# The first FFN projection by tokens, in block products with 512 and 384 moving weight columns, and activations turned on TensorE

## The chip, the cores and the metric

The kernel runs on one core of a Trainium2 chip. A core has a matrix engine (TensorE, PE), three engines for elementwise work (VectorE or DVE, ScalarE or ACT, GpSimd or POOL) and queues for DMA transfers, of which SyncE's (SP) carries nearly all loads here. The engines run side by side and wait for each other through semaphores. The metric is the device time of one execution in microseconds, as the median of several runs.

## What is computed

One layer of a streaming encoder over 512 tokens of 1024 features, in float32. The part that the change touches is the feed-forward network at the end:

```python
    h = h + (g_a * ya + g_b * yb) @ w_o[l]
    hn = rmsnorm(h, norm_ffn_g[l])
    gu = hn @ w_ffn_in[l]
    g, up = jnp.split(gu, 2, axis=-1)
    h = h + (jax.nn.silu(g) * up) @ w_ffn_out[l]
    return rmsnorm(h, final_norm_g)
```

`w_ffn_in` has 1024 rows and 2 x 2816 columns, `w_ffn_out` 2816 rows and 1024 columns. Ahead of it come one combined projection, a gated recurrence with a convolution, and a band attention with 16 heads.

## The kernel before

**Three matmuls for a product.** Each float32 operand is split into a high part (rounded to the type fp32r) and a low part, the rest. A product of two such operands is high x high + high x low + low x high, three matmuls (`mm3`, lines 76 to 78). A split is one ACT copy (line 82) and one DVE subtraction (line 83). A matmul holds a block of 128 x 128 (the stationary operand) and streams the columns of the other (the moving operand), at most 512, through it.

**Block products.** The larger products are cut into 2 x 2 blocks and computed with seven block products instead of eight (Strassen's method in Winograd's form). It needs sums of blocks on both sides, made on DVE, and a few copies and additions of partial results.

**The projection before.** For each pair of 128 features of the gate half ("fg", j = 0, 2 .. 20) and of the up half ("fu"), two loads of 512 KB bring 1024 x 256 weights. `weight_sums` (line 182) makes four sums of 512 elements per partition and splits seven blocks into tiles of the pool `wp` (tag "whl", four buffers) and of others. `block_product` (line 452) runs seven products of 4 x 3 matmuls with the weights held and 256 tokens moving, keeps partial results with ACT (line 460), and adds them on DVE (lines 472 and 473). The results have features on partitions, which is what the second projection wants; SiLU (line 1381) and a multiplication (line 1386) make the activations. The first pair, "fg0" and "fu0", is computed plainly, without blocks, in halves of 256 tokens: `project_half` (line 1297), 8 x 3 matmuls for each of 4 tiles and 2 halves. That covers the norm of the second half of the tokens: `norm_half` (line 526) scales the rows (line 532), turns them on PE (line 543), and writes high parts (line 545, ACT), low parts (line 547, DVE) and the whole values (line 550, ACT) of the features; sums of these blocks (lines 1325 to 1339) are the moving side of the block products. The sums for "fg2" are begun ahead (line 1276).

**What sets the order.** PE runs in an order written by hand from the attention to the norm (`manual_schedule`), and again, with DVE, in the second projection; elsewhere a planner orders each engine by simulated times, except where `keep_in_program_order` fixes an instruction. Weights are prepared ahead by `prefetch`, up to the chunk named by `barrier`. Loads go through SP in order; a raw tile (pool `wp`, three buffers) must be free first.

**Around it.** `v_all` (line 1013) computes the attention's values by tokens: activations are held and 512 weight columns move, in seven block products of 2 x 4 x 3 matmuls, over two weight tiles per kind, of the four "whl" buffers. The output projection `w_o` works in the same way (`o_product`, line 1226); two of its four weight sums, and the parts of two others, are made early, in the recurrence, by `o_weight_sums` (line 353) and kept in DRAM. In the second projection five feature pairs are computed plainly (`plain`, after `split_act`) and six by blocks (`paired`, after `a_first` and `a_sums`).

Of the kernel before, what the change touches and what calls it, by code (L numbers as in the profile page):

```python
# [38 lines left out]
def block_kernel(ctx: ExitStack, tc: tile.TileContext, x, norm_mix_g, w_in, b_merge, rel_table,  # L39
# [54 lines left out]
    strassen = [f"f{w}{j}" for j in range(2, FT, 2) for w in "gu"]  # L94
# [33 lines left out]
    for j in range(0, FT, 2):  # L128
        plan(f"fg{j}", cols(w_ffn_in, j * P))
        plan(f"fu{j}", cols(w_ffn_in, DFF + j * P))  # L130
# [27 lines left out]
    def load(name, k):  # L158
# [4 lines left out]
        pl, bufs = wp, 3  # L163
        if name in strassen and name[0] == "f":
            loads[0] += 1
            pl, bufs = (room[0], 1) if loads[0] % 4 == 0 and loads[0] > 4 else (wp, 3)
        raw = pl.tile([P, n, wide], F32, tag="raw", bufs=bufs, name=f"raw_{name}_{k}")
# [7 lines left out]
    slots, loads = [0], [0]  # L175
    barrier = ["o_w11"]
    room = [None]

    begun = {}
    spare = [None]  # L180

    def weight_sums(name, ahead=False):

        def blocks_of():
            for k in (0, 4):
                if (name, k) not in raws:
                    load(name, k)
            r0, r1 = raws.pop((name, 0)), raws.pop((name, 4))
            return r0[:, :, 0:P], r0[:, :, P:CW], r1[:, :, 0:P], r1[:, :, P:CW]

        if name not in begun:
            a11, a21, a12, a22 = blocks_of()
            s21, s34 = (sums_room.tile([P, 2, 4, P], F32, tag=tag, bufs=1, name=f"{tag}_{name}")
                        for tag in ("s21", "s34"))
            s2, s1, s3, s4 = s21[:, 0], s21[:, 1], s34[:, 0], s34[:, 1]
            first_sum = dve.tensor_add(s1, a21, a22)
            if name == "fu2":

                tc.keep_in_program_order(first_sum)
            dve.tensor_sub(s2, s1, a11)  # L200
            dve.tensor_sub(s3, a11, a21)
            dve.tensor_sub(s4, a12, s2)
        if ahead:
            slots[0] += 1
            o = sums_room.tile([P, 2, 2, 4, P], F32R, tag="whl", bufs=1, name=f"whl_{name}_s2")
            split(o[:, :, 0], o[:, :, 1], s21[:])
            begun[name] = (s34, {"s2": o[:, 0], "s1": o[:, 1]})
            return
        sc = room[0]
        blocks_ = {}  # L210
        if name in begun:

            a11, a21, a12, a22 = blocks_of()
            s34, blocks_ = begun.pop(name)
            s1 = s2 = None
            s3, s4 = s34[:, 0], s34[:, 1]
        for group in ((("a11", a11), ("a12", a12)), (("s2", s2), ("s1", s1)), (("s3", s3), ("s4", s4)), (("a22", a22),)):
            if group[0][0] in blocks_:
                continue
            if name == "fg2" and group[0][0][0] == "a":  # L220

                for key, src in group:
                    o = spare[0].tile([P, 2, 4, P], F32R, tag="act", bufs=13, name=f"whl_{name}_{key}")
                    split(o[:, 0], o[:, 1], src)
                    blocks_[key] = o
                continue
            pl, tag, bufs = sc, "a22", 2
            if len(group) == 2:
                slots[0] += 1
                pl, tag, bufs = (sums_room, "whl", 1) if slots[0] % 5 == 1 else (wp, "whl", 4)  # L230
            o = pl.tile([P, len(group), 2, 4, P], F32R, tag=tag, bufs=bufs, name=f"whl_{name}_{group[0][0]}")
            together = group[0][0] in ("s2", "s3")
            if together:
                split(o[:, :, 0], o[:, :, 1], (s21 if group[0][0] == "s2" else s34)[:])
            for i, (key, src) in enumerate(group):
                if not together:
                    split(o[:, i, 0], o[:, i, 1], src)
                blocks_[key] = o[:, i]
        return blocks_
# [106 lines left out]
    o_sums = {n: dr.tile([2, P, D], F32, name=f"o_t{n}") for n in (1, 2)}  # L346
    o_parts = {n: dr.tile([2, P, 2 * D], F32, name=f"o_hl{n}") for n in (3, 4)}

    def o_block(dst, kh, half, u):
        at = kh * S + u * CW  # L350
        sp.dma_start(out=dst, in_=w_o[at:at + CW, half * S:half * S + S].rearrange("(k p) e -> p k e", p=P))

    def o_weight_sums(pl, u):

        tiles = [pl.tile([P, 2, S], F32R, tag=f"b{n}", name=f"o_b{n}_{u}")[:] for n in range(4)]
        b11, b12, b21, b22 = (f(b) for b in tiles)
        for n, b in enumerate((b11, b12, b21, b22)):
            o_block(b, n // 2, n % 2, u)
# [4 lines left out]
        for n, hi, b in ((1, tiles[1], b12), (2, tiles[3], b22)):  # L363
            sp.dma_start(out=o_sums[n][u], in_=b.rearrange("p k e -> p (k e)"))
        for n, hi, lo in ((3, tiles[1], tiles[0]), (4, tiles[3], tiles[2])):
            act.activation(hi, f(lo), AF.Copy)
            dve.tensor_sub(lo, f(lo), f(hi))
            for part, o in enumerate((hi, lo)):
                sp.dma_start(out=o_parts[n][u][:, part * D:(part + 1) * D], in_=f(o).rearrange("p k e -> p (k e)"))
# [82 lines left out]
    def block_product(name, i, right, c):  # L452
# [6 lines left out]
        def keep(o, src):  # L459
            act.activation(o, src, AF.Copy)  # L460
# [1139 lines left out]
```

## Time and profile before

| What | Value |
|---|---|
| Median of 3 runs | 853.36 us (853.11 to 853.51) |
| The profiled execution | 853.5 us |
| Its span, first to last instruction | 851.7 us |
| Read from HBM | 105.97 MB |

All times of single instructions are of the one profiled execution; its span is 1.8 us shorter than its time as measured from outside. A row of a timeline gives the start of an instruction in the span, its duration in us, the engine, the line of the kernel, the operation, the tiles written and read, and how many followed in a row (x). A row of a window gives for each engine the time in which it was busy and how many instructions touched the window; PEclk is the granted share of TensorE's clock, and the last two columns are the busy share of the DMA engines and GB/s. A row of a group gives busy time and mean duration of one in ns, then the idle time of the engine before these instructions and what ended it. A row of waits names who waited, for whom, and the total, the times and the longest in us.

### The profile page before, as it was taken

Reading aid. Unit: us, or ns where it says so; the run is one execution under the profiler, and the core shown is the slowest. Engines: PE = TensorE matmul, PEld = TensorE weight load, DVE = VectorE, ACT = ScalarE, POOL = GpSimd, SP = SyncE. Lnnn points to the kernel's source line nnn. Section 1 sums busy time; section 2 is a strip of 40 time slices with the busy share of each in tenths; the row PEclk is TensorE's granted clock in tenths of the full one; section 3 lists DMA queues with packets and bytes.
Section 4 is the critical chain, followed back from the end, with each engine's and each line's share of the span. In section 5 each row is a group of like instructions: output and inputs, shape, how many; then the busy total and the mean of one; then the engine's idle time right before and its main releaser. Section 6 shows DMA issues by size and latency. Waiting matters only on the chain.

```text
span 851.7 us, 13103 instructions
## 1 busy us (share of the span) xinstructions
PE 841.7 (99%) x4890; PEld 742.0 (87%) x4890; DVE 662.9 (78%) x1032; ACT 521.0 (61%) x913; POOL 99.8 (12%) x161
## 2 busy tenths in 40 slices
PE   8999999999999999999999999999999999999996
PEld 6988888888888888888888889999999999888885
DVE  6667769777958788887578687898888787798785
ACT  7595848774356688787643477556556557545434
POOL 2412030221110133233000000000000001000000
PEclk9999999999999999999999999999999999999999
DMA  9433386432724433232233861433333333337432
GB/s 293 157 105 118 125 295 247 117 100 90 229 63 146 130 93 100 75 88 62 76 122 118 320 240 49 142 104 120 100 99 105 98 107 104 123 131 239 160 125 99
DMA packets 96670, 115.24 MB, mean 135 GB/s; under 512 B 6520, under 2 KB 78800, under 8 KB 96096
## 3 DMA queue, kind: packets, MB, share of 16 engines
q1 hardware_dynamic: 94976, 110.90, 40.9%
q10 hardware_dynamic: 1232, 2.95, 0.9%
q8 instruction: 38, 0.62, 0.3%
q0 software_dynamic: 400, 0.57, 0.2%
q14 instruction: 24, 0.20, 0.1%
HBM read 105.97 MB, written 8.43 MB: 134 GB/s over the span
## 4 chain that ended last, share of the span: by engine, by line
PE 97%; DVE 1%; ACT 1%; DMA 0%; issue 0%; ACTq 0%; DVEq 0%
PE po_out L76 2%; PE po_out L77 2%; PE po_out L78 2%; PE o L1130 2%; PE p_fu L78 2%; PE p_fg L78 2%; PE p_fg L77 2%; PE p_fg L76 2%; PE p_fu L77 2%; PE p_fu L76 2%; PE pT L1110 2%; PE po_gb L76 2%; PE po_xr L76 2%; PE po_xr L77 2%; PE po_ga L78 2%; PE po_q L76 2%
## 5 line engine op out<-in xcount | busy, mean ns | idle before, releaser
L1099 POOL TENSOR_SCALAR p<-p,rl 128x128 f32<-128x128 f32 (+3 forms) x61 | 37.5, 635 | 16.5 <-DVE rl L1095 15.8
L1094 ACT ACTIVATE p<-p,m 128x128 f32<-128x128 f32 (+1 forms) x64 | 35.5, 555 | 5.2 <-DVE m L1093 4.9
L1371 POOL TENSOR_TENSOR act_lo<-act,act_hi 128x1024 fp32r<-128x1024 f32 x1 | 2.4, 2408 | 299.3 <-ACT act_hi L1370 299.3
L1093 DVE CUSTOM_DVE_ANT_0 p<-s,bias 128x128 f32<-128x128 f32 (+1 forms) x64 | 28.6, 486 | 11.1 <-PE s L1085 9.2
L76 PE MATMUL po_out<-whl_fo,act_hi 128*128 128x512 f32 (+1 forms) x80 | 30.8, 385 | 0.5 <-ACT c_u L460 0.5
L78 PE MATMUL po_out<-whl_fo,act_lo 128*128 128x512 f32 (+1 forms) x80 | 30.7, 384 | 0.0
L77 PE MATMUL po_out<-whl_fo,act_hi 128*128 128x512 f32 (+1 forms) x80 | 30.7, 384 | 0.0
L83 DVE TENSOR_TENSOR whl_fu_s<-s_fu,whl_fu_s 128x1024 fp32r<-128x1024 f32 x20 | 24.2, 1222 | 6.3 <-ACT whl_fu_s L82 6.3
L83 DVE TENSOR_TENSOR whl_fg_s<-s_fg,whl_fg_s 128x1024 fp32r<-128x1024 f32 x20 | 24.1, 1223 | 5.7 <-ACT whl_fg_s L82 5.7
L83 DVE TENSOR_TENSOR pp<-pT,pp 128x384 fp32r<-128x384 f32 (+1 forms) x48 | 26.9, 595 | 2.0 <-ACT pp L82 1.8
L77 PE MATMUL po_xr<-xnT,whl_xr 128*128 128x512 f32 (+1 forms) x80 | 27.7, 353 | 0.0
L77 PE MATMUL po_gr<-xnT,whl_gr 128*128 128x512 f32 (+1 forms) x80 | 27.5, 347 | 0.0
L78 PE MATMUL po_gr<-xnT,whl_gr 128*128 128x512 f32 (+1 forms) x80 | 27.3, 347 | 0.0
L78 PE MATMUL po_xr<-xnT,whl_xr 128*128 128x512 f32 (+1 forms) x80 | 27.2, 346 | 0.0
L76 PE MATMUL po_gr<-xnT,whl_gr 128*128 128x512 f32 (+1 forms) x80 | 27.1, 347 | 0.0
L76 PE MATMUL po_xr<-xnT,whl_xr 128*128 128x512 f32 (+1 forms) x80 | 26.3, 351 | 0.4 <-ACT xnT L658 0.4
L76 PE MATMUL po_k<-xnT,whl_qk 128*128 128x512 f32 x64 | 25.5, 398 | 0.0
L76 PE MATMUL po_q<-xnT,whl_qk 128*128 128x512 f32 x64 | 25.5, 398 | 0.0
L76 PE MATMUL po_ga<-xnT,whl_ga 128*128 128x512 f32 x64 | 25.4, 397 | 0.0
L76 PE MATMUL po_gb<-xnT,whl_gb 128*128 128x512 f32 x64 | 25.2, 394 | 0.0
L78 PE MATMUL po_ga<-xnT,whl_ga 128*128 128x512 f32 x64 | 25.0, 391 | 0.1
L77 PE MATMUL po_ga<-xnT,whl_ga 128*128 128x512 f32 x64 | 25.0, 390 | 0.0
(603 smaller groups left out, 3267.1 us busy)
## 6 DMA issues: line engine op xcount, KB each, us to landing
raw_fg<-in_w_ffn_in_dram SPq DMA_DIRECT2D x24, 512.0 KB, 4.0
raw_fu<-in_w_ffn_in_dram SPq DMA_DIRECT2D x22, 512.0 KB, 3.5
raw_qk<-in_w_in_dram SPq DMA_DIRECT2D x32, 256.0 KB, 3.2
raw_fo<-in_w_ffn_out_dram SPq DMA_DIRECT2D x16, 512.0 KB, 3.4
raw_xr<-in_w_in_dram SPq DMA_DIRECT2D x8, 512.0 KB, 5.6
raw_gr<-in_w_in_dram SPq DMA_DIRECT2D x8, 512.0 KB, 4.3
raw_ga<-in_w_in_dram SPq DMA_DIRECT2D x8, 512.0 KB, 3.8
raw_gb<-in_w_in_dram SPq DMA_DIRECT2D x8, 512.0 KB, 3.7
```

Of the source, the lines that this page charges most:

```text
L76: pe.matmul(o, sh, mh, start=start, stop=False, skip_group_check=parts)
L77: pe.matmul(o, sh, ml, start=False, stop=False, skip_group_check=parts)
L78: pe.matmul(o, sl, mh, start=False, stop=stop, skip_group_check=parts)
L83: dve.tensor_sub(lo, src, f(hi))
L1093: dve.tensor_tensor_reduce(prob[qb][:], scs[qb][:, 0:w], bias[:, S - w:S], -1.0, 3e38, ALU.add, ALU.min, nmax[:, qb:qb + 1])
L1094: act.activation(prob[qb][:], prob[qb][:], AF.Exp, bias=nmax[:, qb:qb + 1], scale=-1.0, accum_out=lsum[:, qb:qb + 1])
L1099: eng.tensor_scalar(prob[qb][:], prob[qb][:], rl[:, qb:qb + 1], 1.0, ALU.mult, ALU.mult)
L1110: pe.transpose(pt[:, at * P:(at + 1) * P], prob[qb][:, kb * P:(kb + 1) * P], ident[:])
L1130: pe.matmul(po[:, S - n:S], st, pp[i][:, part, lo:lo + n], start=kb == 0 and part == 0, stop=kb == NT - 1 and part == 1)
L1371: (dve if i else pool).tensor_sub(lo[:], o[:], f(hi[:]))
```

## The change

The first projection is computed by tokens, like V and `w_o`: activations are held, weights move. The columns of each half are cut into three units, "fg0", "fu0", "fg1" .. "fu2": 1024 columns in the first two, as two sides of 512, and 768 in the last, as two sides of 384. Each unit runs seven kinds of block products, 2 banks x 4 x 3 matmuls each, with `f_weights` preparing one kind ahead: two loads per kind (four for w11, none for t1 and t4), the sums t1 and t2 in tiles of their own, and two splits into two of the four "whl" tiles. Blocks that are used twice are loaded twice.

The first unit has another order of kinds: w11 and w21, which read the first half of the tokens alone, stand first, while the second half is normalised. Its weight sums are made early by the helper that did so for `w_o`: one half after the last group of the recurrence, the other after the first key tile, and kept in DRAM (t1, t2, t3 whole, t4 in parts). The norm of the second half takes its features in the order 4, 6, 0, 2, with a quarter of a product between the groups. The block for the first half of the features and the second half of the tokens is no longer split, since no product reads it; of the first four `mT` tiles only half is split.

SiLU and the multiplication with the up half work on tiles of 128 tokens (`gated`), the multiplication mostly on GpSimd. Then PE turns the activations, four transposes of 128 x 128 per feature tile and one ACT copy, two tiles at a time behind the first four products of the next gate unit, and the last six tiles at the start of the second projection. There the splits of plain pairs 2 to 4 and the tasks for the six block pairs are spread anew.

The core of the difference:

```diff
-    for j in range(0, FT, 2):
-        plan(f"fg{j}", cols(w_ffn_in, j * P))
-        plan(f"fu{j}", cols(w_ffn_in, DFF + j * P))
+    f_units = [f"f{w}{n}" for n in range(3) for w in "gu"]
+    f_first = ("w11", "w21", "t4", "t1", "t2", "w22", "t3")
+    for unit in f_units:
+        for kind in f_first if unit == f_units[0] else v_kinds:
+            plan(f"{unit}_{kind}")
...
+    kept_sums = {(w, n): dr.tile([2, P, D], F32, name=f"{w}_t{n}") for w, n in (("o", 1), ("o", 2), ("f", 1), ("f", 2), ("f", 3))}
+    kept_parts = {(w, n): dr.tile([2, P, 2 * D], F32, name=f"{w}_hl{n}") for w, n in (("o", 3), ("o", 4), ("f", 4))}
...
+        if (w, kind) == ("f", "t4"):
+            hl = [[sums_room.tile([P, 2, S], F32R, tag=f"t{1 + u}{part}", bufs=1, name=f"whl_f_t4_{u}{part}") for part in range(2)]
+                  for u in range(2)]
+            for u in range(2):
+                for part in range(2):
+                    sp.dma_start(out=f(hl[u][part][:]).rearrange("p k e -> p (k e)"), in_=kept_parts[w, 4][u][:, part * D:(part + 1) * D])
+            return lambda part, k: hl[k // 2][part][:, k % 2]
...
+        pl, bufs = (room[0], 1) if f_loads[0] % 4 == 0 and room else (wp, 3)
+        raw = pl.tile([P, 2, S], F32, tag="raw", bufs=bufs, name=f"raw_{unit}_{kind}_{kh}{side}{u}")
+        at, col = kh * S + u * CW, "gu".index(unit[1]) * DFF + int(unit[2]) * 2 * S + side * wide
+        sp.dma_start(out=raw[:, :, 0:wide], in_=w_ffn_in[at:at + CW, col:col + wide].rearrange("(k p) e -> p k e", p=P))
...
+    def f_weights(unit, kind):
+
+        hl = [wp.tile([P, 2, 2, S], F32R, tag="whl", bufs=4, name=f"whl_{unit}_{kind}_{u}")[:, :, :, 0:f_side(unit)]
+              for u in range(2)]
+        for u in range(2):
+            if kind in ("t1", "t4"):
+                src = f_sums[1 if kind == "t1" else 2, u]
+            elif kind == "t2":
+                ins = f_sum(unit, 2, u, f_raw(unit, kind, 1, 1, u), f_sums[1, u])
+                if u == 0:
+                    tc.keep_in_program_order(ins)
+                src = f_sums[2, u]
+            elif kind == "t3":
+                src = f_raw(unit, kind, 0, 0, u)
+                ins = dve.tensor_sub(src, f_sums[2, u], src)
+                if u == 0:
+                    tc.keep_in_program_order(ins)
+            else:
+                src = f_raw(unit, kind, int(kind[1]) - 1, int(kind[2]) - 1, u)
+            split(hl[u][:, 0], hl[u][:, 1], src)
+            if kind == "w11":
+                f_sum(unit, 1, u, f_raw(unit, kind, 0, 1, u), src)
+            if kind == "w21":
+                dve.tensor_sub(f_sums[2, u], src, f_sums[2, u])
...
-        if j in (2, 4):
-            o_weight_sums(obp, j // 2 - 1)
-    ob_stack.close()
+        if j:
+            sums_kept(obp, "oof"[j // 2 - 1], (0, 1, 0)[j // 2 - 1])
...
     k_tile(0)
+    sums_kept(obp, "f", 1)
+    ob_stack.close()
...
-        split_pair(mT[j], ta[j])
+        at = low_ if j < 4 else every
+        split(mT[j][:, 0, at], mT[j][:, 1, at], ta[j][:, at])
...
+    f_rows = {"w11": (0, 0), "w21": (1, 0), "t4": (1, 1), "t1": "s1", "t2": "s2", "w22": "s4", "t3": "s3"}
...
+        for a in of:
+            at = slice(a * P, (a + 1) * P)
+            for k in ks:
+                mm3(banks[a], src[:, 0, k, at], src[:, 1, k, at], w(0, k), w(1, k), start and k == 0, k == 3, parts=True)
...
+            o = sg[2 * half + a, side]
+            if unit[1] == "g":
+                if keep:
+                    dve.tensor_add(o, banks[a], keep[a])
...
+            else:
+                if keep:
+                    dve.tensor_add(keep[a], banks[a], keep[a])
+                (pool if keep and (unit != f_units[-1] or side) else dve).tensor_mul(o, o, keep[a] if keep else banks[a])
...
+            pt = mm_tile(f"pt_act{j}", "t" if n == 2 and i == 2 else "s")
+            for t in range(NT):
+                pe.transpose(pt[:, t * P:(t + 1) * P], sg[t, side][:, i * P:(i + 1) * P], ident[:])
+            act.activation(act_tile(j // 2)[:, j % 2], pt[:], AF.Copy)
...
+    f_product(fx, "fg0", "w11", True)
+    kept(x1, fx)
+    norm_half(x32p, ht, hsq, gf, hn_at, 1, "ffn", f_at, None, first_products, (4, 6, 0, 2), turned_in)
+    f_product(fy, "fg0", "w21", True, of=(1,), ks=(2, 3))
+    gated("fg0", 0, 0, fy, x1)
...
+    x_sum("s1", dve.tensor_add, lambda i: of_x(0, 1, i), lambda i: of_x(1, 1, i))
...
+    f_product(fz, "fg0", "t4", True)
+    kept(y4, fz)
...
+    fz = f_banks("fg0", "t", "t")
+    f_product(fz, "fg0", "t1", True)
+    kept(z1, fz)
...
+        f_product(fx, unit, "w11", True)
+        kept(x1, fx)
+        turn()
+        f_product(fz, unit, "t1", True)
+        kept(z1, fz)
+        turn()
+        f_product(fx, unit, "t2", False)
+        kept(x2, fx)
+        turn()
+        if last:
             split_act(0)
+        f_product(fz, unit, "w22", False)
+        gated(unit, 0, 1, fz, x2)
+        turn()
+        if last:
+            split_act(1)
+        f_product(fx, unit, "t3", False)
+        gated(unit, 1, 1, fx, z1)
+        fy = f_banks(unit, "y", "t")
+        f_product(fy, unit, "w21", True)
+        gated(unit, 0, 0, fy, x1)
+        f_product(fx, unit, "t4", False, 2 if last else 1)
+        gated(unit, 1, 0, fx)
+        if unit[1] == "u":
+            turns += turns_of(n, sg)
+    turn(3)
+    in_order.close()
...
-            spread(todo, 2 if i < plain[-1] else len(todo))
+            if i + 2 in plain:
+                split_act(i + 2)
+            if i == 0:
+                turn(3)
+                sc_stack.close()
+                bt_stack.close()
+                hn_stack.close()
+                ohp.append(ctx.enter_context(pool_of("act_hi", 1, "right")))
+                out_room[0] = ctx.enter_context(pool_of("out", 1, "right"))
+                barrier[0] = None
+            else:
+                spread(todo, 3)
```

358 lines of the change are left out of this document (142 added, 216 removed).

## The prediction, made before the changed kernel was run

> **What bounds the kernel now.** I read the page from its first part down: busy shares, slices, then the waits of TensorE (PE).
>
> ```profile
> PE 841.7 (99%) x4890; PEld 742.0 (87%) x4890; DVE 662.9 (78%) x1032; ACT 521.0 (61%) x913; POOL 99.8 (12%) x161
> ...
> PE   8999999999999999999999999999999999999996
> ```
> ```profile
> PE busy L486 <- DVE eps_t L492: 1.2, 1, 1.2
> PE po_out L76 <- ACT c_u L460: 0.5, 1, 0.5
> PE po_xr L76 <- ACT xnT L658: 0.4, 2, 0.2
> ```
>
> PE is busy in 841.7 of 851.7 us, and nearly all of the rest lies before its first and after its last matmul: the waits add up to a few us in all. So the time is PE's work, and the question is how long PE takes for the new instruction list and whether the others still keep it fed. In a busy PE the mean duration is no price, since neighbours overlap; the price is the step from one start to the next. The windows and the timeline give it:
>
> ```profile
> core 0: us, PE busy (x) PEld busy (x) DVE busy (x) ACT busy (x) POOL busy (x), PEclk, DMA share, GB/s
> 425.00:480.00 55.00, 55.00 (x244) 45.54 (x243) 44.22 (x71) 25.32 (x37) 0.00 (x0) 1.00 0.47 158
> 560.00:720.00 160.00, 160.00 (x1336) 160.00 (x1335) 134.99 (x186) 95.30 (x172) 2.41 (x1) 1.00 0.34 103
> ```
> ```profile
> 494.74 0.39 PE L76 MATMUL o_x<-whl_o_t,ms 128*128 128x512 f32 x1
> ...
> 498.60 0.39 PE L78 MATMUL o_x<-whl_o_t,ms 128*128 128x512 f32 x1
> 498.83 0.27 PE L543 MATMUL pt_ffn_0t<-ident,xs_ffn 128*128 128x128 f32 x1
> ...
> 499.59 0.27 PE L543 MATMUL pt_ffn_2s<-ident,xs_ffn 128*128 128x128 f32 x1
> ...
> 506.42 0.28 PE L76 MATMUL po_f<-hn,whl_fg 128*128 128x256 f32 x1
> ...
> 511.70 0.28 PE L78 MATMUL po_f<-hn,whl_fg 128*128 128x256 f32 x1
> ```
>
> 18 matmuls of 512 columns start within 3.86 us: 3.86/17 = 0.227 us each. 45 of 256 columns within 5.28 us: 0.120 each. Eight transposes: 0.76/7 = 0.109. The windows agree (160 us over some 1334 matmuls in the FFN, 55 over some 242 in an all-512 stage), at a full granted clock. So two matmuls of 256 cost 0.240 where one of 512 does the same columns in 0.227: about 13 ns of each matmul do not scale with its columns, and the weight-load row says the same (160.00 of 160 us busy in the FFN, 45.54 of 55 in the other stage). That is what this change can win.
>
> **The change, part by part.** *Matmuls.* Before: 20 column pairs of 7x4x3 = 84 matmuls and the first pair plain with 192, all of 256 columns: 1872 x 0.120 = 224.6 us. After: 6 units of 7 products x 2 banks x 4 x 3 = 168 matmuls; four units of 512 columns (672) and two of 384 (336). For 384 the attention has a step:
>
> ```profile
> 305.20 0.34 PE L1084 MATMUL s<-kh,q 128*128 128x384 f32 x1
> 305.37 0.34 PE L1085 MATMUL s<-kl,q 128*128 128x384 f32 x1
> 305.55 0.39 PE L1084 MATMUL s<-kh,q 128*128 128x512 f32 x1
> ```
>
> 0.17 to 0.18; I take the middle of the other two steps, 0.1735. 672 x 0.227 + 336 x 0.1735 = 152.5 + 58.3 = 210.8. Saved: 13.8 us.
>
> *Turning.* The products now come out with tokens on partitions, the second projection wants features there: 22 feature tiles x 4 = 88 transposes are new.
>
> ```profile
> 280.18 1.09 PE pT L1110 x10
> 289.26 1.12 PE pT L1110 x10
> ```
>
> In the attention ten in a row take 1.09 to 1.12 on the chain, so 0.11 each with the change of kind: 88 x 0.11 = 9.7 us. They come in some 12 groups; a group between matmuls may cost up to 0.05 more, 0.6. The transposes of the norm are as many as before.
>
> *A stall that goes.* At the end of the FFN PE waits 0.5 us for the last eviction (second row of the waits). Now the turn of three tiles and a plain output group, 4 x 6 x 0.227 = 5.4 us, stand between the last product and what needs it. What is late next is the multiply of the last bank, two of under 0.7 us: covered. -0.5.
>
> Sum: -13.8 + 9.7 + 0.6 - 0.5 = **-4.0 us**, as long as PE stays fed.
>
> *Feeding PE: DVE and ACT.* A 512 unit (168 x 0.227 = 38.1 us) needs on DVE 14 low parts and 8 sums of 1024 and 6 adds out of PSUM, in an up unit 2 multiplies besides:
>
> ```profile
> L83 DVE TENSOR_TENSOR whl_fu_s<-s_fu,whl_fu_s 128x1024 fp32r<-128x1024 f32 x20 | 24.2, 1222 | 6.3 <-ACT whl_fu_s L82 6.3
> L473 DVE TENSOR_TENSOR c_u<-q_fu,keepa_fu 128x512 f32<-128x512 f32 x10 | 6.9, 688 | 3.1 <-PE q_fu L78 2.1 <-ACT keepa_fu L460 0.8
> L82 ACT ACTIVATE whl_fu_s<-s_fu 128x1024 fp32r<-128x1024 f32 x20 | 20.8, 1054 | 4.2 <-PE q_fg L78 2.2 <-PE q_fu L78 1.7 <-DVE s_fu L202 0.2
> ```
>
> 22 x 1.22 + 6 x 0.69 = 31.0 (up: 32.4) of 38.1, 81 to 85%; in the window above DVE already works 134.99 of 160 (84%) without a single PE wait. ACT: 14 x 1.05, 6 copies, 8 SiLUs or 8 evicted turns of about 0.6: some 23 to 28 of 38. No fuller than now, so the shares cost nothing; the order can. Four weight tiles hold two kinds, so a kind can be split only while the one before it runs: 5.4 us (384: 4.2) for high, low, high, low: 1.05 + 2 x 1.22 = 3.5 at best, 5.9 where two sums stand in between. The V stage runs the same scheme without a PE wait. I take 0; the other end is rival C.
>
> *GpSimd.* 16 multiplies and the low parts of activation pairs 0 to 2 (one there before) go to POOL. They wait for adds, and a turn asks for them one product later. Nearest row:
>
> ```profile
> L773 POOL TENSOR_TENSOR xch<-xc,xch 128x512 fp32r<-128x512 f32 x8 | 11.7, 1466 | 23.1 <-issue 13.0 <-ACT xch L772 10.1
> L83 DVE TENSOR_TENSOR whl_ga<-raw_ga,whl_ga 128x1024 fp32r<-128x1024 f32 x8 | 11.9, 1497 | 2.4 <-ACT whl_ga L82 2.4
> ```
>
> 1.5 us each, hidden. In the stage where POOL does this, DVE's low parts take 1.50 instead of 1.22. The Trainium skill, "GPSIMD Engine Reference" (section "Specifications"), has the reason: GpSimd shares SBUF interfaces with VectorE, with contention where a VectorE instruction has two SBUF inputs; the row agrees. Six such multiplies in an up unit slow perhaps 8 low parts by 0.28: 2.2 us of DVE, from 85 to 91%. Cost 0 with the slack, part of rivals B and C.
>
> *DMA.*
>
> ```profile
> raw_fg<-in_w_ffn_in_dram SPq DMA_DIRECT2D x24, 512.0 KB, 4.0
> raw_fu<-in_w_ffn_in_dram SPq DMA_DIRECT2D x22, 512.0 KB, 3.5
> ```
>
> From the second unit on 12 raw loads per unit instead of one pass: 5 x 12, and 16 for the first, against these 46. 6.3 MB in 38.1 us is 165 GB/s, against 103 above, over three raw tiles and every fourth in a tile of its own. The stage before the FFN shows what PE stands (next rows). Cost 0.
>
> *Sums kept early.* The first unit's weight sums are made in the recurrence and after the first keys: 8 loads, 10 stores, 10 DVE and 2 ACT instructions, with SP's later weight loads queued behind stores that wait for DVE. The same helper already does this for w_o, twice.
>
> ```profile
> 105.00:125.00 20.00, 20.00 (x90) 16.57 (x89) 14.49 (x17) 10.77 (x15) 7.77 (x4) 1.00 0.86 316
> 165.00:200.00 35.00, 35.00 (x156) 29.00 (x155) 23.23 (x29) 24.91 (x35) 6.96 (x10) 1.00 0.40 119
> 460.00:500.00 40.00, 40.00 (x182) 33.20 (x182) 29.22 (x48) 19.53 (x32) 0.00 (x0) 1.00 0.72 267
> ```
>
> At 105 to 125 the chip does exactly that for w_o, at 316 GB/s, and PE is busy throughout. At 165 to 200 DVE has 11.8 us free for 10 x 1.22 = 12.2 us; the rest delays V's sums a little, needed 40 us later. Cost 0; cover gone, about 1 us.
>
> *The FFN's start.* Before, 72 matmuls (8.6 us) cover the second half's norm, now 24 x 0.227 = 5.4.
>
> ```profile
> 506.22 0.68 DVE L200 TENSOR_TENSOR s_fg<-s_fg,raw_fg 128x512 f32<-128x512 f32 x1
> ...
> 507.67 0.68 DVE L202 TENSOR_TENSOR s_fg<-raw_fg,s_fg 128x512 f32<-128x512 f32 x1
> ...
> 509.11 1.22 DVE L83 TENSOR_TENSOR whl_fg_s<-s_fg,whl_fg_s 128x1024 fp32r<-128x1024 f32 x1
> ...
> 510.51 1.40 DVE L532 TENSOR_SCALAR xs_ffn<-h,rs_ffn 128x1024 f32<-128x1024 f32 x2
> ...
> 517.57 1.42 DVE L1325 TENSOR_TENSOR sum_t<-x 128x512 f32<-128x512 f32 x2 [0.17 <-ACT x L550]
> ...
> 520.12 1.22 DVE L1339 TENSOR_TENSOR bt<-sum_t,bt 128x1024 fp32r<-128x1024 f32 x1 [1.12 <-ACT bt L1338]
> ```
>
> PE would reach the transposes at 511.4, the scaled rows are done at 511.9; but the two sums and the split for "fg2" ahead of them on DVE, 2.6 us, are gone. Cost 0 to 0.5.
>
> ```profile
> 515.47 0.27 PE L543 MATMUL pt_ffn_2s<-ident,xs_ffn 128*128 128x128 f32 x1
> ```
>
> From these transposes (515.7) to a split sum (521.3) are 5.6 us; after the change PE has, from its last transposes, 6 + 24 matmuls, 6.8 us, before it needs s1. Covered by about 1 us. One of the norm's four blocks is no longer split, nor half of the first four mT tiles: a little less for ACT and DVE, off PE's path.
>
> *The output's start.* Low parts of pairs 3 and 4 (2.4 us of DVE; pair 2's on POOL) move behind the FFN, and twelve tasks spread over four plain groups, not five.
>
> ```profile
> 740.00:760.00 20.00, 20.00 (x90) 16.57 (x89) 18.02 (x34) 10.30 (x15) 0.00 (x0) 1.00 0.45 151
> ```
>
> DVE is at 18.02 of 20 there; 2.4 us more in five groups of 5.4 still fits, since what comes last is first read by the sixth. SP's loads from "fo0_3" on open one group later and have two more to land. Cost 0; cover gone, up to 2.4.
>
> **The sum.** The profiled execution took 853.5 us (span 851.7), the median shown is 853.36; the difference is nothing here. 853.4 - 4.0 = **849.4 us**.
>
> **The rivals.** A measurement of this kernel tells about 0.2% from no change, 1.7 us. *A, the forecast:* PE stays fed, 849.4, alone 848 to 851. For it: 84% of DVE and no wait now. Chance 0.65.
>
> *B, the covers are a little short:* 0.5 at the scaled rows, 1.5 at s1, 0.3 in each of five units: +3.5, so 852.9, from 851 to 854. For it: the cover at s1 is about 1 us, and six POOL multiplies per up unit slow DVE. Against it: PE is at 160.00 of 160 us today with engines as full. 0.20, mostly within 0.2%.
>
> *C, the two-kind weight buffer becomes the bound (slower):* if sums cannot run ahead, a kind with two sums takes 5.9 us against 5.4 of product; four of seven kinds in five units are such: 20 x 0.45 = 9, so 858.4. It decides once raw weights land later than the start of the product before, so that sum and split stand in a row; landing takes 3.5 to 4.0 us by the page's DMA issues and the raw tiles come free some 5 us ahead. Against it, V. 0.12.
>
> *D, the change does not do what its shapes say:* a transpose holds PE for its duration, 0.275 us, instead of its step: 88 x 0.275 = 24.2, so 863.9. Against it the rows of ten in 1.1 us. The Trainium skill, "TensorE: Matmul & The Clock Gate", Part 4, gives a transpose about 275 ns in a kernel's context; the duration agrees, the step here is 0.11. The same page, "Back-to-back issue gap", puts N/2.4 + 2.5 ns on a warm matmul: by it, as an estimate, 1872 x 109.2 = 204.4 against 672 x 215.8 + 336 x 162.5 = 199.6, a saving of 4.8 alone, and with the transposes the change would lose. As a mechanism of this kernel: were the part that does not scale 2.5 instead of 13 ns, the saving would shrink to about a third and the sum be +5, 858. The steps of 0.120 and 0.227 speak against it. Both 0.03.
>
> **How the numbers follow.** Faster: A and a quarter of B, 0.70. Within 0.2% (851.7 to 855.1): the rest of B, 0.15. Slower: C and D, 0.15. The range: down to 848.0 (transposes at 0.109, no cost of a group, 384 at 0.170), up to 853.8 with nearly all of B; C and D left out.
>
> **What would show it.** Right: matmuls of the projection at 128x512 in steps of 0.227, the stage some 4 us shorter, no PE waits by the projection's products; DVE at about 80% there. B would show as PE waits on the split sums or on norm transposes; C as PE waits on weight tiles, once per heavy kind; D as steps of transposes near 0.275. Wrong would be a wait that grows before the FFN, by the stores in SP's queue.

## The result, and the profile after

The kernel after takes **859.75 us** (median of 7 runs, 858.30 to 863.98); the kernel before took 853.40 beside it (853.11 to 853.88). The ratio is 1.0082 (95% interval 1.0063 to 1.0101): slower by 0.8%, where 849.4 was forecast. The profiled execution of after is the longest of the seven, 863.98 us, with a span of 862.2.

First the busy row, what HBM moved, and PE's waits of the kernel after (who waits, for whom: total, times, longest in us).

```profile
PE 844.7 (98%) x4114; PEld 712.7 (83%) x4114; DVE 662.3 (77%) x972; ACT 519.7 (60%) x864; POOL 140.9 (16%) x179
...
HBM read 122.75 MB, written 13.67 MB: 158 GB/s over the span
```
```profile
PE v_z L77 <- DVE whl_v_t L83: 3.5, 1, 3.5
PE o_z L78 <- DVE ms L83: 1.9, 1, 1.9
PE fu_x L77 <- DVE whl_fu_t L83: 1.6, 1, 1.6
PE fg_x L77 <- DVE whl_fg_t L83: 1.3, 2, 0.7
...
PE fg_y L77 <- DVE whl_fg_w L83: 0.4, 1, 0.4
```

The five rows shown are new, six waits in all, each for a low part that DVE makes (one more new row, of 0.3 us in the attention, is not). The two largest lie in stages whose products the change does not touch: V (`v_z`) and the output projection (`o_z`). DVE is no fuller than before (77% against 78%): what changed is when it gets to the piece that PE wants. The 0.5 us for `c_u` is gone, as forecast.

Three landmarks cut the span: the first matmul of the o stage (the output projection `w_o`), the first transpose of the FFN's norm, the last matmul. Their rows in PE's timeline, of before and then of after:

```profile
466.18 0.39 PE L76 MATMUL o_x<-whl_o_w,mT 128*128 128x512 f32 x1
...
844.84 0.28 PE L78 MATMUL po_last<-whl_fo,act_lo 128*128 128x256 f32 x1
```
```profile
472.53 0.39 PE L76 MATMUL o_x<-whl_o_w,mT 128*128 128x512 f32 x1
...
509.01 1.04 PE L494 MATMUL pt_ffn<-ident,xs_ffn 128*128 128x128 f32 x8
...
855.39 0.28 PE L78 MATMUL po_last<-whl_fo,act_lo 128*128 128x256 f32 x1
```

With the row at 498.83 that the prediction shows: up to the o stage +6.35, in the o stage 36.48 against 32.65 (+3.83), from the norm to the end 346.38 against 346.01 (+0.37). So in this execution 10.2 us are lost before the changed products begin, and their gain of 4 does not show either. The medians are some 6 us apart: the other executions of after lost less. Each part is followed back to what holds DVE.

**V.** DVE's timeline of after, and then PE's (start, duration, and in brackets the idle time before and what ended it):

```profile
245.86 0.16 DVE L1049 RECIPROCAL rl<-l 128x4 f32<-128x4 f32 x1
249.60 1.41 DVE L272 TENSOR_TENSOR raw_v_t<-v_t,raw_v_t 128x1024 f32<-128x1024 f32 x1 [3.58 <-DMA raw_v_t<-in_w_in_dram]
250.93 1.21 DVE L83 TENSOR_TENSOR whl_v_t<-v_t,whl_v_t 128x1024 fp32r<-128x1024 f32 x1
```
```profile
248.28 0.39 PE L76 MATMUL v_z<-whl_v_t,v_s1h 128*128 128x512 f32 x1
252.20 0.50 PE L77 MATMUL v_z<-whl_v_t,v_s1h 128*128 128x512 f32 x1 [3.53 <-DVE whl_v_t L83]
...
253.22 0.63 PE L77 MATMUL v_z<-whl_v_t,v_s1h 128*128 128x512 f32 x1
253.65 0.63 PE L78 MATMUL v_z<-whl_v_t,v_s1l 128*128 128x512 f32 x1
```

The low part that PE waits for (250.93) needs nothing that is late. It stands behind the sum for **t3** (line 272), which no product wants before three more have run, and that sum waits 3.58 us for a raw tile that was still landing. Behind the wait PE's steps are 0.43 instead of 0.227, at a granted clock of 0.53 (window 252.5 to 256.0 us): half clock. What made the stage tight is, by the trace, a row in ACT's timeline 40 us earlier:

```profile
208.20 0.59 ACT L907 ACTIVATE kh<-po_k 64x512 fp32r<-64x512 f32 x1 [6.18 <-DMA f_hl<-f_b]
```

A copy of the second key tile waits 6.18 us for the store of the last kept sums of the first unit, whose memory it takes over.

**The o stage.** DVE's timeline, and two rows of the DMA issues from 455 to 530 us (count, KB each, median us to landing):

```profile
475.21 0.68 DVE L83 TENSOR_TENSOR mT<-za,mT 128x512 fp32r<-128x512 f32 x1
480.70 0.69 DVE L1193 SCALAR_TENSOR_TENSOR h<-o_x,h 128x512 f32<-128x512 f32 x1 [4.81 <-PE o_y L77]
...
487.26 0.68 DVE L83 TENSOR_TENSOR ms<-za,ms 128x512 fp32r<-128x512 f32 x1
```
```profile
whl_f_t<-f_hl SPq DMA_DIRECT2D x4, 512.0 KB, 7.1
h<-in_x_dram ACTq DMA_DIRECT2D x4, 512.0 KB, 10.8
```

The first h add waits 4.81 us, and the `ms` splits that the t1 product wants stand behind it. The bracket names a step of `o_y`, which this add does not read, and the `o_x` product that it does read had ended by 478.2 us. So it was another input: h, whose loads take a median of 10.8 us to land beside the four new loads of t4 parts. They were issued from 472.7 us on, and the quickest took 7.9 us, which gives 480.6.

**The FFN.** Its waits (1.6, 1.3, 0.4) are for low parts in fg1, fg2 and fu2.

### The profile page after: what moved, and what is told of

It reads as the page before. It is cut to its first block, busy times and chain, and to the rows that moved or that the text cites. A ratio compares the mean times of both kernels' runs of the same rounds, so it can differ in the third digit from the quotient of the medians.

```text
span 862.2 us, 11589 instructions
## 1 busy us (share of the span) xinstructions
PE 844.7 (98%) x4114; PEld 712.7 (83%) x4114; DVE 662.3 (77%) x972; ACT 519.7 (60%) x864; POOL 140.9 (16%) x179
## 3 DMA queue, kind: packets, MB, share of 16 engines
HBM read 122.75 MB, written 13.67 MB: 158 GB/s over the span
## 4 chain that ended last, share of the span: by engine, by line
PE 68%; DVE 13%; DMA 11%; ACT 4%; issue 4%; DVEq 0%; ACTq 0%; SPq 0%
DMA raw_fu_w<-in_w_ffn_in_dram 3%; PE po_out L76 2%; PE po_out L77 2%; PE po_out L78 2%; PE o L1084 2%; PE pT L1064 2%; DMA raw_fg_w<-in_w_ffn_in_dram 2%; PE po_ga L78 2%; PE po_ya L76 2%; PE po_ya L77 2%; PE po_ya L78 2%; PE po_ga L76 2%; PE po_ga L77 2%; DMA raw_fu_t<-in_w_ffn_in_dram 1%; PE po_xr L77 1%
## 5 line engine op out<-in xcount | busy, mean ns | idle before, releaser
L1282 POOL TENSOR_TENSOR sg<-sg,keep_fu_x 128x512 f32<-128x512 f32 (+1 forms) x10 | 18.3, 1853 | 240.4 <-DVE keep_fu_x L1281 240.4
L1053 POOL TENSOR_SCALAR p<-p,rl 128x128 f32<-128x128 f32 (+3 forms) x61 | 42.7, 718 | 15.6 <-DVE rl L1049 14.8
L83 DVE TENSOR_TENSOR whl_fo<-raw_fo,whl_fo 128x1024 fp32r<-128x1024 f32 x16 | 20.7, 1303 | 8.0 <-ACT whl_fo L82 8.0
L82 ACT ACTIVATE whl_fu_t<-t_fu 128x1024 fp32r<-128x1024 f32 (+1 forms) x18 | 17.6, 985 | 13.0 <-PE fu_x L78 8.7
L76 PE MATMUL po_ga<-xnT,whl_ga 128*128 128x512 f32 x64 | 25.5, 398 | 0.0
L1275 ACT ACTIVATE sg<-sg 128x512 f32<-128x512 f32 (+1 forms) x20 | 11.9, 596 | 22.4 <-DVE sg L1274 22.0
L78 PE MATMUL po_ga<-xnT,whl_ga 128*128 128x512 f32 x64 | 25.0, 391 | 0.1
## 6 DMA issues: line engine op xcount, KB each, us to landing
raw_qk<-in_w_in_dram SPq DMA_DIRECT2D x32, 256.0 KB, 3.1
```

Of the source, the lines that this page charges most:

```text
L76: pe.matmul(o, sh, mh, start=start, stop=False, skip_group_check=parts)
L78: pe.matmul(o, sl, mh, start=False, stop=stop, skip_group_check=parts)
L82: act.activation(hi, src, AF.Copy)
L83: dve.tensor_sub(lo, src, f(hi))
L1053: eng.tensor_scalar(prob[qb][:], prob[qb][:], rl[:, qb:qb + 1], 1.0, ALU.mult, ALU.mult)
L1275: ins = act.activation(o, o if keep else banks[a], AF.Silu)
```

## The experiments

Unless said otherwise each is an edit of the changed kernel. Ratios are against the kernel before, run beside each (medians 853.59 to 853.67), with 95% intervals. Line numbers of the edited kernels differ a little. "Pinned" means held in program order. The times between the landmarks, from the same three rows of each profile, in us:

| Kernel | median | profiled execution | start to o stage | o stage | norm to end |
|---|---|---|---|---|---|
| before | 853.4 | 853.5 | 466.18 | 32.65 | 346.01 |
| after | 859.75 | 863.98 | 472.53 | 36.48 | 346.38 |
| 1 sums early | 856.53 | 855.22 | 466.36 | 34.67 | 345.60 |
| 2 t4 late | 859.05 | 859.21 | 470.00 | 32.65 | 347.95 |
| 3 before + sums | 858.56 | 857.41 | 470.33 | 32.64 | 346.01 |
| 4 = 1 and 2 | 855.23 | 855.24 | 466.40 | 32.64 | 347.62 |
| 5 = 4, low parts on DVE | 853.46 | 853.10 | 466.66 | 32.64 | 345.20 |
| 6 = 4, t1 sums pinned | 849.16 | 849.01 | 466.04 | 32.64 | 341.74 |
| 7 = 5, multiplies on DVE | 851.82 | 851.07 | 466.23 | 32.64 | 343.58 |
| 8 = 5 and 6 | 849.59 | 849.36 | 466.38 | 32.64 | 341.75 |
| 9 = 6, sums late | 856.21 | 856.21 | 473.19 | 32.65 | 341.75 |
| 10 = 9, t3 sums pinned | 850.16 | 850.46 | 467.46 | 32.65 | 341.75 |
| 11 three pins alone | 850.26 | 850.25 | 467.18 | 32.72 | 341.76 |
| 12 two pins alone | 851.35 | 851.77 | 467.52 | 33.92 | 341.76 |

The landmarks are of one execution each. That of after is the longest of its seven and that of run 1 the shortest of its six, so between these two the landmarks show a gain of 8.8 us where the medians show 3.2.

**1. The sums one slot earlier.**

```diff
-        if j:
-            sums_kept(obp, "oof"[j // 2 - 1], (0, 1, 0)[j // 2 - 1])
+        sums_kept(obp, "ooff"[j // 2], (0, 1, 0, 1)[j // 2])
+    ob_stack.close()
...
-    sums_kept(obp, "f", 1)
-    ob_stack.close()
```

> The changed kernel with the kept sums one slot earlier in the recurrence (w_o's after the first and second column pair, the first unit's after the third and fourth), so that none stands behind the first keys. Theory: V's stage is late because kh of the second key tile waits for the stores of the last kept sums (6.2 us in the changed kernel's profile), DVE's queue stands behind it, and PE waits 3.5 us and then runs at half clock for 3.3 us. Then the shift of the last attention tile, +6.35 against the kernel before, falls to within 1 us of 0, the row of PE waiting on whl_v_t goes, and the time is 853 to 855 against 859.75. Rival 1: the sums cost what they cost in whatever slot, by DVE time and DMA traffic: the wait turns up on a weight tile of the recurrence, and the time stays at 858 to 861. Rival 2: V's weights are late because of the memory that is released later, not by the stores: no change either.

Measured: 856.53 (1.0035, 1.0023 to 1.0047). V's wait is gone and the start is back at +0.18, so in V's stage the slot is what cost, not the work. The time stays above the expected 853 to 855 since the o stage (next fence) and the FFN still wait.

```profile
PE o_z L78 <- DVE ms L83: 1.7, 1, 1.7
PE fu_x L77 <- DVE whl_fu_t L83: 1.6, 1, 1.6
```

**2. The t4 loads later.**

```diff
-                    sp.dma_start(out=f(hl[u][part][:]).rearrange("p k e -> p (k e)"), in_=kept_parts[w, 4][u][:, part * D:(part + 1) * D])
+                    tc.keep_in_program_order(
+                        sp.dma_start(out=f(hl[u][part][:]).rearrange("p k e -> p (k e)"), in_=kept_parts[w, 4][u][:, part * D:(part + 1) * D]))
```

> The changed kernel with the four loads of the kept t4 parts held in program order on SP's queue, behind the raw loads of the first unit's w11 and w21, so that they are issued after 500 us and not at 471 to 481. Theory: they share the DMA with the loads of h, whose landing goes from about 6 to 8 to 11 us, and so delay the h adds on DVE and the ms split that PE waits for (1.9 us, then half clock for 3.3 us). Then that wait goes, the shift between attention and the first norm transposes (+4.0) falls to within 1 us of 0, and the time is 855 to 857 against 859.75. Rival: DVE is late there by itself (its queue in order, not the landing of h): the wait stays and the time is 859 to 861, or more if t4 now lands too late for its own product.

Measured: 859.05 (1.0062, 1.0047 to 1.0077). The o stage is back at 32.65, its wait is gone, and h lands in 5.6 us again (median): the mechanism holds. The median misses the expected 855 to 857: V's wait of 3.1 us is still there, and the FFN waits more than before (347.95).

**3. The sums alone, in the kernel before.** The helper of the change is copied for the first unit's sums and called in the changed kernel's two slots:

```diff
+        if j == 6:
+            f_weight_sums(obp, 0)
...
     k_tile(0)
+    f_weight_sums(obp, 1)
+    ob_stack.close()
```

> The kernel before, its FFN untouched, with the changed kernel's extra kept sums alone (first unit: 8 loads, 10 stores, 10 DVE and 2 ACT instructions, in the same two slots), stored and never read. Theory: these alone make V's stage late: 853.4 + 5 to 6.5 = 858 to 860. Rival: they are hidden, as the prediction had it at cost 0: 853 to 854.

Measured: 858.56 (1.0056, 1.0042 to 1.0070), **+5 us** for work that nothing reads. PE waits 2.2 us at the same place of V, and DVE's timeline has the same order: the t3 sum waits 4.01 us, the low part behind it.

```profile
247.51 1.31 DVE L338 TENSOR_TENSOR raw_v_t<-v_t,raw_v_t 128x1024 f32<-128x1024 f32 x1 [4.01 <-DMA raw_v_t<-in_w_in_dram]
248.75 1.21 DVE L83 TENSOR_TENSOR whl_v_t<-v_t,whl_v_t 128x1024 fp32r<-128x1024 f32 x1
```

**4. Both.** The edits of 1 and 2.

> The edits of the first two runs together: sums one slot earlier and the t4 loads late. Theory: both stalls before the FFN go, and what is left is the FFN's own gain less its waits: -4.0 predicted, +0.2 measured from the first norm transposes to the first add of the output, so 853.5 with the FFN as it runs now, 849.5 if its waits were a consequence of the late start. Rival: the two stalls are not independent of the rest, and something else comes late: over 856.

Measured: 855.23 (1.0022, 1.0013 to 1.0032). Everything ahead of the norm is as before; the FFN keeps 1.6 us more than before instead of 4 less. So its waits are its own. The time is 1.7 us above the larger of the two that were expected. Its rows, DVE first, then GpSimd:

```profile
622.85 1.23 DVE L351 TENSOR_TENSOR t_fu<-raw_fu_w,raw_fu_w 128x1024 f32<-128x1024 f32 x1 [1.29 <-DMA raw_fu_w<-in_w_ffn_in_dram]
623.99 1.22 DVE L83 TENSOR_TENSOR whl_fg_t<-t_fg,whl_fg_t 128x1024 fp32r<-128x1024 f32 x1
...
689.01 0.96 DVE L351 TENSOR_TENSOR t_fu<-raw_fu_w,raw_fu_w 128x768 f32<-128x768 f32 x1 [0.23 <-DMA raw_fu_w<-in_w_ffn_in_dram]
689.88 3.16 DVE L83 TENSOR_TENSOR whl_fg_w<-raw_fg_w,whl_fg_w 128x768 fp32r<-128x768 f32 x1
```
```profile
689.62 2.60 POOL L1370 TENSOR_TENSOR act_lo<-act,act_hi 128x1024 fp32r<-128x1024 f32 x1 [21.91 <-ACT act_hi L1369]
```

Two suspects. The sum `t_fu` is for the next unit's t1; it waits for its raw tile, and the low part of this unit's t4 weights, which PE is out of, stands behind it. And a low part of DVE takes 3.16 us instead of 0.96 while GpSimd makes one. (The expectation for run 7 below counts ten multiplies on GpSimd; the trace of run 4 has sixteen, as forecast.)

**5 to 8. The suspects apart.** From run 4: 5 puts GpSimd's low parts of activations on DVE, 6 holds the t1 sums in program order, 7 is 5 with the gated multiplies on DVE too, 8 is 5 and 6. The edits of 5, of 6 and what 7 adds:

```diff
-        (dve if i > 2 else pool).tensor_sub(lo[:], o[:], f(hi[:]))
+        dve.tensor_sub(lo[:], o[:], f(hi[:]))
```
```diff
-                f_sum(unit, 1, u, f_raw(unit, kind, 0, 1, u), src)
+                tc.keep_in_program_order(f_sum(unit, 1, u, f_raw(unit, kind, 0, 1, u), src))
```
```diff
-                (pool if keep and (unit != f_units[-1] or side) else dve).tensor_mul(o, o, keep[a] if keep else banks[a])
+                dve.tensor_mul(o, o, keep[a] if keep else banks[a])
```

> The fourth run (both stalls before the FFN gone, 855.23) with the low parts of activation pairs 0 to 2 on DVE instead of GpSimd. Theory: in the last two units a DVE instruction stands still as long as GpSimd makes such a low part (DVE's low part takes 3.16 us and a sum 2.00 us beside them, where others of the same size take 0.96), and these 3.2 us are what PE waits for at the end of fg2 (+1.0) and at fu2's t2 (+1.9). Then both waits go, and the time is 852.5 to 853.5, although DVE now has 3 x 1.22 us more to do. Rival 1: what is late there is the landing of the raw weights (3.2 us from issue); then the waits stay and the time is 855 to 856. Rival 2: DVE has no room for 3.7 us more: 856 to 857.

> The fourth run with the next unit's t1 sums held in program order on DVE, behind the splits of this unit's t4 weights. Theory of this run: at the end of fg1 DVE's queue stands 1.2 and 1.3 us for a raw tile of the next unit that is still landing, and the split of fg1's t4 weights, which PE wants, stands behind it (PE +1.7); with the sums behind the splits this wait goes: 853.3 to 854, unless the raw tiles now come free too late. Rival: raw tiles are what is short (four of 4 KB, each reloaded 3 to 5 us after it comes free): a sum made later frees its raw tile later, the wait moves into the next unit, and the time is 855 to 857.

> The fifth run's kernel with the ten gated multiplies of GpSimd on DVE too, so that GpSimd does nothing in the FFN. Theory: a multiply of GpSimd holds DVE up for a part of its 1.85 us as well; DVE's low parts then all take 1.22, and DVE does the ten multiplies in 0.69 each: the time is at most that of the fifth run, 852 to 853.5. Rival, the prediction's: the contention of the multiplies is hidden, and moving them costs as much as it brings: within 0.5 us of the fifth run.

> The edits of the fifth and the sixth run together. If the FFN's waits have two separate causes, GpSimd's low parts (2.9 us of PE) and the order of DVE's queue (1.7 us), both go and the time is near 851; if they are one shortage, of DVE time or of raw tiles, the sum of the two gains is not reached: 853 or more. Before takes 853.6.

Measured: 5 853.46 (0.9997, 0.9988 to 1.0006), 6 **849.16** (0.9951, 0.9939 to 0.9964), 7 851.82 (0.9980, 0.9971 to 0.9989), 8 849.59 (0.9952, 0.9939 to 0.9964). The pin alone brings 6 us, far more than its own expectation, and taking the low parts from GpSimd besides brings nothing. Run 5 falls in its range, though one of the two waits that it was to remove is only halved (fu2, 1.6 to 0.8); run 7 comes out 1.6 under run 5, so the rival that moving the multiplies changes nothing falls. DVE's order is enough to cure the waits. It is not their whole cause: with nothing left on GpSimd (run 7) the order still costs 1.8 us between the norm and the end (343.58 against 341.74), and the other 4 of the 5.9 that separate run 4 from run 6 need GpSimd's work beside it. In run 6 the low part that PE wants comes first, GpSimd still holds DVE up (2.22 us for a low part of 0.96, at fu2), and PE does not notice:

```profile
615.76 1.23 DVE L83 TENSOR_TENSOR whl_fg_t<-t_fg,whl_fg_t 128x1024 fp32r<-128x1024 f32 x1 [1.65 <-ACT whl_fg_t L82]
...
617.50 1.22 DVE L83 TENSOR_TENSOR whl_fg_t<-t_fg,whl_fg_t 128x1024 fp32r<-128x1024 f32 x1
...
703.38 2.22 DVE L83 TENSOR_TENSOR whl_fu_t<-t_fu,whl_fu_t 128x768 fp32r<-128x768 f32 x1 [1.10 <-ACT whl_fu_t L82]
```
```profile
560.00:720.00 160.00, 160.00 (x811) 142.26 (x810) 129.62 (x131) 90.62 (x124) 32.88 (x17) 1.00 0.50 155
```

The last row is run 6's window of the FFN, to be read beside the one of before in the prediction: PE busy in all 160 us again, with 811 matmuls in place of 1336. So GpSimd counts only where the order has used up the slack already: that is what 5 and 7 took back, by the medians 1.8 and 3.4 us of the 6.

**9. V's stall alone.** Run 6 with the sums back in the changed kernel's slots.

> The changed kernel with the t4 loads late and the t1 sums pinned, but the kept sums in their own late slots: of the three causes only V's is left. Theory: the three add up, so 849.2 + 5 (the run of before with the extra sums alone) = 854 to 855, with the wait of PE on whl_v_t at V's t1 and none in the FFN. Rival: the FFN only ran without waits because it started on time; then waits come back in it, 856 or more.

Measured: 856.21 (1.0015, 1.0001 to 1.0030), scattered from 851.23 to 856.90 over 11 runs. The FFN stays at 341.75, so its waits do not depend on V's, and the rival falls; the profiled run has V's wait in full (next row) and +7.0 at the start. The median is 1 to 2 us above the expectation, and the costs do not simply add: V's stall costs 7.0 here by the medians, while taking it from the changed kernel (run 1) brought 3.2. How large it is changes from run to run.

```profile
PE v_z L77 <- DVE whl_v_t L83: 3.5, 1, 3.5
```

**10. V's t3 sums held in program order.** Run 9 with

```diff
-                dve.tensor_sub(src, v_t2[u], src)
+                tc.keep_in_program_order(dve.tensor_sub(src, v_t2[u], src))
```

> The ninth run with V's t3 sums held in program order on DVE, nothing moved. Theory, the same for all three stalls: a DVE instruction that the planner set early waits at the head of the in-order queue for a DMA that lands later than planned, and the split that PE wants stands behind it. In V's stage that is the t3 sum (waits 3.6 us for its raw tile at 246 us of the changed kernel's profile, the t1 split behind it). Then pinning it takes the wait down from 3.5 to under 1 us although the kept sums stay where they are: 849.5 to 851. Rival: DVE and ACT are simply behind by the 6.2 us that the stores cost (key copies and V's sums run that much later); then the pin moves the wait to another tile and the time stays at 853.5 to 855.

Measured: 850.16 (0.9961, 0.9949 to 0.9974). The copy of the key tile still waits 6.15 us for the store (ACT's timeline), and PE now 0.7 (its waits). The start is 1.3 us above before's instead of 7.0. V stands the late sums; the rival, that it is late whatever DVE's order, falls.

```profile
208.73 0.59 ACT L908 ACTIVATE kh<-po_k 64x512 fp32r<-64x512 f32 x1 [6.15 <-DMA f_hl<-f_b]
```
```profile
PE v_z L77 <- DVE whl_v_t L83: 0.7, 1, 0.7
```

**11 and 12. Order alone.** 11 is the changed kernel with the pins of 6 and 10 and a third; nothing is moved, t4 is loaded early. 12 leaves the third pin out.

```diff
-            dve.scalar_tensor_tensor(hs, banks[a][:], 0.5, hs, ALU.mult, ALU.add)
+            ins = dve.scalar_tensor_tensor(hs, banks[a][:], 0.5, hs, ALU.mult, ALU.add)
+            if half == cc == 0:
+                tc.keep_in_program_order(ins)
```

> The changed kernel with three edits of DVE's order alone (t1 sums of the FFN, t3 sums of V, the first two h adds of the o stage, each held in program order); the kept sums stay late and the t4 loads early. Theory: all three stalls are a matter of what stands ahead in DVE's queue, so all three go: 849 to 851, though the loads of h and t4 still share the DMA. Rival: where DMA time is short (h beside t4) or the sums late, order alone does not help: 852 to 856.

> The eleventh run without its third pin: t1 sums of the FFN and t3 sums of V held in program order, the h adds of the o stage free, t4 early. Theory: the o stage's wait is its own, as in the first run, where V was cured too and PE still waited 1.7 us for a split of ms; so that wait comes back and the time is 851.5 to 852.5 against 850.26. Rival: with V on time the order of the o stage comes out well by itself, and the third pin does nothing: 849.5 to 850.5.

Measured: 11 **850.26** (0.9960, 0.9948 to 0.9973), 12 851.35 (0.9973, 0.9961 to 0.9984). Three pins on DVE bring 9.5 us and turn the change from slower to faster than before. In 11 h still lands slowly beside t4 (first row, DMA issues from 455 to 530 us), but DVE has done one weight split more ahead of the h add than in run 12 and waits 2.32 for h in place of 4.81:

```profile
h<-in_x_dram ACTq DMA_DIRECT2D x4, 512.0 KB, 10.7
```
```profile
471.38 1.22 DVE L83 TENSOR_TENSOR whl_o_t<-raw_o_t,whl_o_t 128x1024 fp32r<-128x1024 f32 x1
474.92 0.69 DVE L1193 SCALAR_TENSOR_TENSOR h<-o_x,h 128x512 f32<-128x512 f32 x1 [2.32 <-DMA h<-in_x_dram]
```

Without the third pin (12) the wait is back, at 0.9. The median is 1.1 us longer than in 11, a little under the expected 851.5 to 852.5, and the o stage takes 33.92 in place of 32.72; the intervals of the two runs overlap, so the traces decide here, not the medians:

```profile
PE o_z L78 <- DVE ms L83: 0.9, 1, 0.9
```

## Why the prediction was wrong

**Matmuls, Turning, A stall that goes: right.** With PE fed (runs 6, 8 to 12) the part from the norm to the end takes 341.74 to 341.76 against 346.01: -4.27, where the sum said -4.0. The steps are those of the working: over that part of run 6's trace the median step is 0.227 for 512 columns, 0.173 for 384 and 0.109 for a transpose; rival D falls, and with it the gap of 2.5 ns. That -4.27 lies so near -4.0 is in part luck, since three small terms nearly cancel. A group of transposes costs about 0.01 us and not 0.05 (in run 6, at 513.21 us, four transposes and the matmul behind them take 0.67, where the steps alone give 0.66). The stall that goes was worth 0.7 and not 0.5 (in the trace of before the steps around it, from 736.46 us, are 0.75 and 0.33 in place of 0.12 and 0.23). And the FFN's start, below, cost 0.6 where 0 was taken. Without its waits the change is worth what the forecast gave: 849.16 beside 849.4.

**Sums kept early: the step that failed most.** Cost 0, "cover gone, about 1 us". Run 3 measures 5 us for these instructions by themselves. The working counted DVE's time (10 x 1.22 beside 11.8 us free) and said that V's sums are needed 40 us later. It did not follow what the stores hold: the second key tile takes the memory of the last sums, waits 6.2 us for their store, and by the trace that delay uses up V's slack. Already in the kernel before the t3 sum waited 3.86 us ahead of the same low part, early enough for PE not to see it; "the rest delays V's sums a little" should have led to that row.

```profile
241.24 1.23 DVE L338 TENSOR_TENSOR raw_v_t<-v_t,raw_v_t 128x1024 f32<-128x1024 f32 x1 [3.86 <-DMA raw_v_t<-in_w_in_dram]
242.39 1.22 DVE L83 TENSOR_TENSOR whl_v_t<-v_t,whl_v_t 128x1024 fp32r<-128x1024 f32 x1
```

**DMA: wrong by its place.** Cost 0 was argued for the FFN, where it holds (155 GB/s, no wait in run 6). But the four t4 loads wait for nothing the FFN makes, go out in the o stage, and double the landing time of h (5.8 us before, 10.8 after, from the issues of 455 to 495 and to 530 us). Price: 3.83 us in the profiled run of after, 2.0 in run 1.

**Feeding PE: right in the shares, wrong in the order.** "No fuller than now, so the shares cost nothing; the order can": it did, with about 6 us (run 4 to run 6), and rival C came nearest, with 9. That its 858.4 lies near the measured 859.75 is luck, since in the profiled execution 10.2 us are lost ahead of the FFN, where C sees nothing. Its mechanism was half of it. Sums and splits do stand in a row when raw weights land late, but the row is not forced by the buffers of two kinds: the same buffers feed PE without a wait once a sum that nobody wants yet no longer stands ahead of the split. That V "runs the same scheme without a PE wait" was no evidence: V only had slack.

**GpSimd: right where DVE's order leaves slack.** There it is hidden, as costed (run 8 is run 6 within its scatter). The sizes were too small: in the trace of after a multiply takes 1.85 us and not 1.5, DVE's low parts beside one take up to 1.71 and not 1.50, and what GpSimd's own low parts do to DVE, the 3.16 us of run 4, had no term. **The FFN's start** cost about 0.6, near its upper end of 0.5, but not where the working looked. In run 6 the first transposes of the second half follow in step at 511.38, so the scaled rows are in time; the third group, at 515.34, is late, and the weight loads of these transposes wait 0.8 us in all for ACT's copies of the whole values (`x`). That is all that came of rival B's places; **the output's start** shows no wait. "A wait that grows before the FFN" was named as what would be wrong; it came by DVE's queue, not by SP's.

**What stays open.** That the 6.2 us for the store, rather than the rest of the sums' work, make V late is read from the trace of after: DVE starts V's sums at 211.50 us there and at 199.85 before, and 4.54 us of the difference it stands idle for that key copy. The wait was not taken away by itself. Run 9's scatter of 5.7 us goes with the granted clock: the two shortest executions, 851.23 and 851.61, had a mean of 0.999 and 0.998, the seven from 855.8 up 0.994 to 0.996. But 851.23 is 2.1 us above run 6, less than the 3.5 us that PE waited in the profiled execution, so the wait itself changes too; why is not known.

## What to carry to other kernels

When a change adds loads or stores, look in the trace of before for in-order engines that already wait for a DMA ahead of work that the bound engine wants: such a wait is hidden only as long as everything ahead keeps its time, and a busy share does not show it. Pin an instruction whose data comes late behind the ones whose results are due first; here three pins brought 9.5 us, and 16.8 MB more read from HBM (122.75 in place of 105.97) then cost PE one wait of 0.4 us, in V (run 11). Before a stage is priced at nothing, follow its stores to whoever takes over their memory.

## What the runs showed of the hardware

**Short waits and the clock.** PE's waits of 1.9 us (o stage, after), 2.2 (run 3) and 3.5 (V, after, and run 9) were each followed by some 3 to 5 us of steps of 0.43, at a granted clock of 0.50 to 0.53; waits of 1.7 (run 1) and 3.1 (run 2) were not. So the length of the wait alone does not decide, and a wait of 1.9 us can cost nearly as much again (the nine steps behind it, at 0.2 us more than usual each). The Trainium skill, "TensorE: Matmul & The Clock Gate" (Part 1), describes a free-running window of 3.4 us and half clock after an idle one, with the advice to avoid idle gaps of over about 3.4 us. A window that lies where it happens to lie would fit that equal waits differ, but no run here shows it; the 1.9 and 2.2 us are well under its figure, and there the measurement decides.

**GpSimd holds DVE up to its end.** While GpSimd makes a low part of 128x1024 (2.4 to 2.6 us), a DVE subtraction with two SBUF inputs that starts beside it ends about 0.8 us after GpSimd does, as if nearly all of its usual 0.96 us came only then. In run 4 (rows above) GpSimd ends at 692.22 and DVE at 693.04, after 3.16 us; in run 6 at 704.79 (next row) and 705.60, after 2.22. An addition that reads PSUM for one input is not held up: beside the low part at 686.52 in run 6 it takes its usual 0.56. The Trainium skill, "GPSIMD Engine Reference" (Specifications), names contention for DVE instructions with two SBUF inputs; the rows show its extent.

```profile
702.37 2.42 POOL L1370 TENSOR_TENSOR act_lo<-act,act_hi 128x1024 fp32r<-128x1024 f32 x1 [13.45 <-issue]
```
